# A gated delta stage with projections of 256 columns and a copy of them on the chip

## The chip, the cores and the metric

The kernel is one decoder layer for one sequence of 4096 tokens with a width of 1024, in float32, on one core of a Trainium2 chip. The metric is the device time of one execution in microseconds (us). TensorE multiplies matrices into PSUM; VectorE (DVE), ScalarE (ACT) and GpSimd (POOL) do the rest; GpSimd works in SBUF alone here; SyncE (SP) issues most DMAs.

## The reference, cut to what matters

The layer normalises the input, projects it, mixes the tokens by two kinds of heads (retention, and a gated delta rule), projects back, and runs a mixture of experts. The change touches the projections of the gated delta heads and the short convolution behind them:

```python
def causal_dwconv(x, w):          # CONV_WIDTH = 4 taps per channel, over time
    k = w.shape[0]
    return lax.conv_general_dilated(x, w[:, None, :].astype(x.dtype), window_strides=(1,), padding=((k - 1, 0),),
                                    dimension_numbers=('NWC', 'WIO', 'NWC'), feature_group_count=x.shape[-1])

h = modulate(rmsnorm(x, norm1_w[l]), shift1, scale1)
proj = h @ w_in[l]                # d_q, d_k, d_v: 512 columns each of the result
qkv = jax.nn.silu(causal_dwconv(jnp.concatenate([d_q, d_k, d_v], axis=-1), conv_w[l]))
cq, ck, cv = jnp.split(qkv.astype(jnp.float32), 3, axis=-1)
dn = gated_delta_rule(dq, dk, heads(cv, DN_HEADS), g, beta)   # dq, dk: cq, ck normalised per head
```

Each output of the convolution needs the projected value of its own token and of the three tokens before it; ahead of the first token stand zeros.

## The kernel before, in words

The kernel runs in four phases. `phase_a` makes the conditioning rows and the normalised, transposed activations, and computes the retention heads. It writes the activations to two tensors in device memory, `hh_d` and `hl_d` (a high part and the rest; a product is three matmuls: high x high, high x low, low x high). These have 4 columns more than tokens; the first 4 are filled with zeros from the tile `z4` (lines 276 to 279). `phase_b`, the stage of the change, computes the gated delta heads. `phase_c` applies the gates, the output projection and the router, `phase_d` the experts.

In `phase_b` the tokens go in 16 groups of G = 256, two chunks of 128 each. `dn_proj` does the projections of a group. The channels are on the partitions: 12 blocks of 128 channels (k, then q, then v), and for each block 24 matmuls (8 slices of the width by three products) accumulate in one PSUM tile `pjB`, with the weights stationary and the activations moving. The group's activations come from `load_h`: 8 DMAs per group into tiles under the tag "h" with 10 buffers, 260 columns each, that is the 256 tokens of the group and 4 columns ahead of them. The projection is thus computed for 260 columns, and the convolution reads its four shifted windows of 256 columns straight from PSUM: ScalarE scales two of them (lines 527 and 528), VectorE multiplies and adds the other two (line 530), GpSimd adds the last two partial sums (line 532), and after two blocks ScalarE applies Silu (line 537). There are three PSUM tiles under the tag "pj".

`dn_early` and `dn_late` do the delta rule of a group. `dn_early` makes the decay (`ru` on GpSimd, `pd` on TensorE, `dt`), the products of the keys (`pG`), and the inverse of the triangular matrices, of which 31 steps of two operations each run on VectorE (lines 600 and 602). Its blocks pass through device memory (`dgo`, `dgi`). `dn_late` combines the inverse blocks (`px`) and carries the state from chunk to chunk (`pP`, `pu`, `pkv`, `poB`).

The order of the work: the generators of a group are cut into steps, and `PROJ`, `EARLY` and `LATE` give each step a place, 12 places per group, so that the late steps of a group lie beside the projections of the next. That is the order in which the program is written. The final order on each engine is made by the framework's scheduler, which works through this program with a simulated timeline; each engine then runs its list strictly in order, and waits are semaphores. A tile with one buffer is written again when all readers of its last content are through.

Of the kernel before, what the change touches and what calls it, by code (L numbers as in the profile page):

```python
# [9 lines left out]
F32 = mybir.dt.float32  # L10
# [3 lines left out]
AF = mybir.ActivationFunctionType  # L14
ALU = mybir.AluOpType
# [4 lines left out]
P = 128  # L20
D = 1024
KD = D // P
H = 4
EPS = 1e-6
NE = 32
G = 256
GT = G // P
# [26 lines left out]
class Kern:  # L54
# [150 lines left out]
    def phase_a(self):  # L205
        tc, nc, T = self.tc, self.nc, self.T
        with tc.tile_pool(name="A", bufs=2) as p, ExitStack() as sctx:
# [21 lines left out]
            for g in range(self.NG):  # L229
                tiles = range(g * GT, (g + 1) * GT)  # L230
                if (g * GT) % 4 == 0:
                    n = min(4, self.NT - g * GT)
# [14 lines left out]
                for k2 in range(KD // 2):  # L247
                    pt = self.psum([P, 2, G], "pt", "tp")
                    for a in range(2):
                        for j, t in enumerate(tiles):  # L250
                            k = 2 * k2 + a
                            nc.tensor.transpose(pt[:, a, j * P:(j + 1) * P], xs[t][:, k * P:(k + 1) * P], self.ident)
                    hf = p.tile([P, 2, G], F32, name="hf", bufs=2)
                    for a in range(2):
                        k = 2 * k2 + a
                        nc.vector.tensor_scalar(hf[:, a], pt[:, a], self.sc1[:, k:k + 1], self.sh1[:, k:k + 1],
                                                op0=ALU.mult, op1=ALU.add)
# [5 lines left out]
                b = (g - min(2, self.NG - 8 // nb)) * nb  # L263
# [9 lines left out]
            nc.tensor.transpose(pc[:, :48], cwr, self.ident[:48, :48])  # L273
            self.cw = self.cp.tile([P, 4, 12], F32, name="cw")
            nc.vector.tensor_copy(self.cw, pc[:, :48].rearrange("p (w b) -> p w b", w=4))
            z4 = p.tile([P, KD, 4], F32, name="z4", bufs=1)
            nc.vector.memset(z4, 0.0)
            for d in (self.hh_d, self.hl_d):
                nc.sync.dma_start(d[:, 0:4].rearrange("(k p) n -> p k n", p=P), z4)

            self.bw = {nm: self.wblock(wi[:, c:c + 512], nc.sync) for nm, c in (("k", 2560), ("q", 2048), ("v", 3072))}
            sctx.close()
# [161 lines left out]
    def phase_b(self):  # L444
        tc, nc, T = self.tc, self.nc, self.T
        with tc.tile_pool(name="B", bufs=2) as p:
            wp = p
            hh0 = self.load_h(p, 0)

            def scalars():  # L450
                self.dn_scalars(p, p)
                self.Sd = p.tile([P, H, P], F32, name="Sd", bufs=1)
                nc.vector.memset(self.Sd, 0.0)
                self.Vb = self.wtile("Vb", F32)[:, 0:D].rearrange("p (h i) -> p h i", h=GT * H)
                nc.gpsimd.memset(self.Vb, 0.0)
                self.Tb = p.tile([64, 2 * H, 64], F32, name="Tb", bufs=1)
                nc.gpsimd.memset(self.Tb, 0.0)
                self.dgo = [self.dp.tile([32, 1024], F32, name=f"dgo{i}") for i in range(2)]
                self.dgi = [self.dp.tile([32, 1024], F32, name=f"dgi{i}") for i in range(2)]
                yield  # L460

            def next_weights():
                wi = self.w_in[0]
                self.gz = []
                for c in (1536, 3584):
                    self.gz.append(self.wblock(wi[:, c:c + 512], nc.sync))
                    yield
                self.dnw = self.xp.tile([P, 1], F32, name="dnw", bufs=1)
                nc.sync.dma_start(self.dnw, self.dn_norm_w.rearrange("o p -> p o"))
                self.wo = [self.wo_block(0)]  # L470
                yield

            steps = [(2.5, 0, 0, 0, scalars())]
            nw = next_weights()
            steps += [(12 * self.NG + 1 + i, 3, 0, i, nw) for i in range(3)]
            st_ = {}
            for g in range(self.NG):
                st_[g] = {}
                for kind, gen, at in ((2, self.dn_proj(p, g, st_[g], None if g else hh0), self.PROJ),
                                      (1, self.dn_early(p, g, st_[g]), self.EARLY),  # L480
                                      (0, self.dn_late(p, g, st_[g]), self.LATE)):
                    for i, o in enumerate(at):
                        steps.append((12 * g + o, kind, g, i, gen))
            for s in sorted(steps, key=lambda s: s[:4]):
                next(s[4], None)
# [11 lines left out]
    def load_h(self, p, g):  # L497

        nc = self.nc
        n = G + 4  # L500
        hh, hl = [], []
        for k2 in range(KD // 2):
            for dst, src, nm in ((hh, self.hh_d, "hhB"), (hl, self.hl_d, "hlB")):
                a = self.xp.tile([P, 2, n], F32R, name=nm, tag="h", bufs=10)
                nc.sync.dma_start(a.bitcast(F32), src[2 * k2 * P:(2 * k2 + 2) * P, g * G:g * G + n].rearrange(
                    "(a p) n -> p a n", p=P))
                dst += [a[:, 0], a[:, 1]]
        return hh, hl

    def dn_proj(self, p, g, st, hh=None):  # L510

        nc = self.nc
        hh, hl = hh or self.load_h(p, g)
        yield
        for b2 in (2, 3, 0, 1, 4, 5):
            cv = self.xp.tile([P, 2, G], F32, name="cv", tag="x0", bufs=2)
            for a in range(2):
                b = 2 * b2 + a
                pj = self.psum([P, G + 4], "pjB", "pj")
                for k in range(KD):  # L520
                    wh, wl = (w[:, b % 4 * P:(b % 4 + 1) * P] for w in self.bw["qkv"[b // 4]][k])
                    nc.tensor.matmul(pj, wh, hh[k], start=(k == 0), stop=False)  # L522
                    nc.tensor.matmul(pj, wh, hl[k], start=False, stop=False)  # L523
                    nc.tensor.matmul(pj, wl, hh[k], start=False, stop=(k == KD - 1))  # L524
                w = [self.cw[:, i, b:b + 1] for i in range(4)]
                t0 = p.tile([P, G], F32, name="cv0", bufs=2)
                nc.scalar.activation(cv[:, a], pj[:, 4:4 + G], AF.Copy, scale=w[3])
                nc.scalar.activation(t0, pj[:, 1:1 + G], AF.Copy, scale=w[0])  # L528
                for i in (2, 1):
                    nc.vector.scalar_tensor_tensor(cv[:, a], pj[:, 1 + i:1 + i + G], w[i], cv[:, a], op0=ALU.mult,  # L530
                                                   op1=ALU.add)
                nc.gpsimd.tensor_tensor(cv[:, a], cv[:, a], t0, op=ALU.add)  # L532
                if a == 0:
                    yield
            nm = "qkv"[b2 // 2] + "T"
            st[nm, b2 % 2] = o = p.tile([P, 2, G], F32, name=nm, bufs=4)
            nc.scalar.activation(o, cv, AF.Silu)
            yield

    def dn_early(self, p, g, s):  # L540
        nc = self.nc
# [5 lines left out]
        for c in range(GT):  # L547
# [9 lines left out]
            nc.gpsimd.tensor_tensor(dt[c], dt[c], self.ui[:, None, :].to_broadcast(sh), op=ALU.mult)  # L557
            s["dt", c] = dt[c]
            yield
        sk = p.tile([P, GT, H], F32, name="sk", bufs=2)  # L560
        for c in range(GT):
            pG.append(self.psum(sh, "pG", "tp"))
            for h in range(H):
# [8 lines left out]
        rk, irk, b, nb = (p.tile([P, GT, H], F32, name=n, bufs=2) for n in ("rk", "irk", "b", "nb"))  # L572
# [6 lines left out]
        for c in range(GT):  # L579
            for h in range(H):  # L580
                nc.vector.scalar_tensor_tensor(at[:, 4 * c + h], pG[c][:, h], nb[:, c, h:h + 1], dt[c][:, h],
                                               op0=ALU.mult, op1=ALU.mult)
# [14 lines left out]
        for j in range(31):  # L597
            n, m = j // 4 + 1, 31 - j
# [11 lines left out]
    def dn_late(self, p, g, s):  # L610
        nc = self.nc
# [6 lines left out]
        fl = lambda t: t.rearrange("p c h -> p (c h)")  # L618
        V, T, at = self.Vb, self.Tb, s["at"]
        kt, vv, sq, o = {}, {}, {}, {}  # L620
        rq = p.tile([P, GT, H], F32, name="rq", bufs=2)
        ms = p.tile([P, GT, H], F32, name="msB", bufs=2)

        def f_sq(c):
# [962 lines left out]
```

## Time and profile before

| What | us |
|---|---|
| Median of 3 runs (lowest, highest) | 4122.11 (4122.01, 4122.9) |
| The profiled execution's own time | 4121.5 |
| Span of the profile | 4119.7 |
| TensorE busy in the span (share) | 3911.6 (95%) |
| VectorE busy (share) | 2467.8 (60%) |
| ScalarE busy (share) | 1587.3 (39%) |
| GpSimd busy (share) | 1525.5 (37%) |
| Mean granted TensorE clock | 0.981 of full speed |

All times within the profile count from the start of the span. The gated delta stage lies from about 787 to 1725 us. An engine counts as busy while an instruction of it runs. Matmuls overlap: the recorded duration of one is longer than the distance to the start of the next, and a busy TensorE is a stream without gaps, not one at its peak. "Idle before" is the time in which an engine had nothing to run, and the name behind it is what ended it.

### The profile page before, as it was taken

What the parts mean: (1) busy time and instruction counts of PE and PEld (TensorE: products, weight loads), DVE (VectorE), ACT (ScalarE), POOL (GpSimd) and SP (SyncE); (2) the same over time, 40 slices, a digit from 0 to 9 for tenths busy, and PEclk for the clock granted to TensorE, in tenths of its full rate; (3) what the DMA queues carried; (4) which work ended last, traced back from release to release, by engine and by line L of the source; (5) the groups of instructions that cost most, each with busy time, mean ns of one, the idle gap of its engine ahead of it and who ended that gap; (6) DMA issues with size and microseconds to landing.
All of it is one profiled execution on the core that took longest, in us unless ns stands there. A gap on an engine that the chain in (4) does not pass through costs nothing.

```text
span 4119.7 us, 73091 instructions
## 1 busy us (share of the span) xinstructions
PE 3911.6 (95%) x27074; PEld 3515.6 (85%) x27074; DVE 2467.8 (60%) x6437; ACT 1587.3 (39%) x3298; POOL 1525.5 (37%) x2133
## 2 busy tenths in 40 slices
PE   5999999999999999979999999699999999999997
PEld 4888889899999999968888888598888888888886
DVE  6555543577778777742222222557777777777785
ACT  3433443444544444421122211234444444444453
POOL 2333334234443344222333333433333443454442
PEclk9999999999999999989999999799999999999999
DMA  6443322422222222453333333346666675666673
GB/s 194 137 128 123 98 91 89 115 59 74 58 60 66 74 61 60 118 158 120 118 123 123 123 123 111 119 142 209 204 225 226 216 237 193 232 209 206 225 233 125
DMA packets 459759, 577.48 MB, mean 140 GB/s; under 512 B 97296, under 2 KB 361720, under 8 KB 459400
## 3 DMA queue, kind: packets, MB, share of 16 engines
q1 hardware_dynamic: 411112, 464.72, 36.4%
q0 software_dynamic: 45632, 102.64, 7.4%
q10 hardware_dynamic: 2656, 5.42, 0.4%
q8 instruction: 214, 3.51, 0.4%
q14 instruction: 145, 1.19, 0.1%
HBM read 458.94 MB, written 166.78 MB: 152 GB/s over the span
## 4 chain that ended last, share of the span: by engine, by line
PE 77%; DVE 8%; DMA 8%; issue 3%; ACT 2%; SPq 1%; POOL 1%; DVEq 0%; POOLq 0%; ACTq 0%
PE ph L1410 5%; PE ph L1411 5%; PE ph L1409 5%; PE pjB L523 4%; PE pjB L522 4%; PE pjB L524 4%; PE py L1502 3%; PE py L1503 3%; PE py L1504 3%; PE pgz L291 3%; PE pgz L292 3%; PE pgz L290 3%; PE poC L291 3%; PE poC L292 3%; PE poC L290 3%
## 5 line engine op out<-in xcount | busy, mean ns | idle before, releaser
L1410 PE MATMUL ph<-xl,whD 128*128 128x240 f32 (+7 forms) x2048 | 588.2, 288 | 3.5 <-DVE xl L72 3.2
L1409 PE MATMUL ph<-xh,whD 128*128 128x240 f32 (+7 forms) x2048 | 580.1, 289 | 11.6 <-DVE ssD L1330 6.5
L1411 PE MATMUL ph<-xh,wlD 128*128 128x240 f32 (+7 forms) x2048 | 586.4, 288 | 0.0
L71 ACT ACTIVATE whD<-rawD 128x1024 fp32r<-128x1024 f32 x384 | 400.9, 1056 | 316.0 <-PE py L1503 125.9
L72 DVE TENSOR_TENSOR wlD<-rawD,whD 128x1024 fp32r<-128x1024 f32 x384 | 460.9, 1218 | 35.1 <-ACT whD L71 33.2
L522 PE MATMUL pjB<-hhB,whi 128*128 128x260 f32 x1536 | 443.1, 291 | 9.5 <-DVE cv L530 4.2
L523 PE MATMUL pjB<-hlB,whi 128*128 128x260 f32 x1536 | 440.7, 288 | 6.3 <-DMA hlB<-hl_d 6.1
L524 PE MATMUL pjB<-hhB,wlo 128*128 128x260 f32 x1536 | 440.8, 288 | 0.0
L1409 PEld LDWEIGHTS ph<-xh,whD 128*128 128x128 f32 x2048 | 388.9, 191 | 17.6 <-DVE ssD L1330 7.1
L1410 PEld LDWEIGHTS ph<-xl,whD 128*128 128x128 f32 x2048 | 391.1, 191 | 8.2 <-DVE xl L72 5.3
L1411 PEld LDWEIGHTS ph<-xh,wlD 128*128 128x128 f32 x2048 | 390.9, 191 | 1.9
L522 PEld LDWEIGHTS pjB<-hhB,whi 128*128 128x128 f32 x1536 | 289.0, 189 | 13.9 <-DMA hhB<-hh_d 4.5
L523 PEld LDWEIGHTS pjB<-hlB,whi 128*128 128x128 f32 x1536 | 290.3, 189 | 10.7 <-DMA hlB<-hl_d 8.3
L524 PEld LDWEIGHTS pjB<-hhB,wlo 128*128 128x128 f32 x1536 | 290.1, 189 | 1.6
L532 POOL TENSOR_TENSOR cv<-cv,cv 128x256 f32<-128x256 f32 x192 | 142.0, 740 | 399.2 <-DVE Xd L602 140.5
L1502 PE MATMUL py<-whD,hh 128*128 128x512 f32 (+4 forms) x640 | 259.5, 405 | 12.4 <-DVE hh L69 7.6
L1503 PE MATMUL py<-wlD,hh 128*128 128x512 f32 (+4 forms) x640 | 252.8, 395 | 0.0
L1504 PE MATMUL py<-whD,hl 128*128 128x512 f32 (+4 forms) x640 | 245.9, 399 | 4.6 <-DVE hl L72 4.3
L946 DVE TENSOR_TENSOR xC<-poC,xC 128x512 f32<-128x512 f32 x64 | 44.2, 691 | 329.6 <-PE poC L292 329.6
L1537 POOL DMA_INDIRECT acc_d<-ag,to x80 | 112.2, 1403 | 345.9 <-DVE ag L1510 257.9
L530 DVE SCALAR_TENSOR_TENSOR cv<-pjB,cw,cv 128x256 f32<-128x256 f32 x384 | 183.1, 479 | 78.8 <-ACT cv L528 71.5
L290 PE MATMUL pj<-whi,hh 128*128 128x512 f32 x512 | 205.8, 402 | 6.0 <-ACT whi L71 6.0
(449 smaller groups left out, 10234.4 us busy)
## 6 DMA issues: line engine op xcount, KB each, us to landing
rawD<-in_w_dram SPq DMA_DIRECT2D x384, 512.0 KB
wa<-in_w_ada_dram SPq DMA_DIRECT2D x48, 512.0 KB
hhB<-hh_d SPq DMA_DIRECT2D x64, 260.0 KB
hlB<-hl_d SPq DMA_DIRECT2D x64, 260.0 KB
acc_d<-xC SPq DMA_DIRECT2D x32, 520.0 KB
wraw<-in_w_in_dram SPq DMA_DIRECT2D x32, 512.0 KB
hh_d<-hh SPq DMA_DIRECT2D x16, 1024.0 KB
hl_d<-hl SPq DMA_DIRECT2D x16, 1024.0 KB
```

Source lines behind the costliest of these rows:

```text
L71: nc.scalar.activation(hi, src, AF.Copy)
L72: (e_lo or nc.vector).tensor_tensor(lo, src, hi.bitcast(F32) if hasattr(hi, "bitcast") else hi, op=ALU.subtract)
L290: nc.tensor.matmul(out, a, hi, start=(k == 0), stop=False)
L522: nc.tensor.matmul(pj, wh, hh[k], start=(k == 0), stop=False)
L523: nc.tensor.matmul(pj, wh, hl[k], start=False, stop=False)
L524: nc.tensor.matmul(pj, wl, hh[k], start=False, stop=(k == KD - 1))
L1409: nc.tensor.matmul(ph[nm], hi, xh[:, k, 0:n], start=(k == 0), stop=False)
L1410: nc.tensor.matmul(ph[nm], hi, xl[:, k, 0:n], start=False, stop=False)
L1411: nc.tensor.matmul(ph[nm], lo, xh[:, k, 0:n], start=False, stop=(k == KD - 1))
L1502: nc.tensor.matmul(py[i], a, hi, start=(k == 0), stop=False)
L1503: nc.tensor.matmul(py[i], a, lo, start=False, stop=False)
L1504: nc.tensor.matmul(py[i], b, hi, start=False, stop=(k == 3))
```

## The change

The projection is computed for the group's own 256 tokens. The last three projected columns of each block are kept in the tile `tail` (12 blocks of 3 columns) for the next group; it starts as zeros. Each PSUM tile is copied once by ScalarE into a tile `pjs` in SBUF with one buffer, behind three columns that GpSimd copies in from `tail`; GpSimd then copies the last three columns out to `tail`. The four windows of the convolution are read from `pjs`. The zero columns in device memory are no longer written, `load_h` reads 256 columns, and the small tiles `sk` and `rq` have one buffer in place of two.

```diff
@@ phase_a
-            z4 = p.tile([P, KD, 4], F32, name="z4", bufs=1)
-            nc.vector.memset(z4, 0.0)
-            for d in (self.hh_d, self.hl_d):
-                nc.sync.dma_start(d[:, 0:4].rearrange("(k p) n -> p k n", p=P), z4)
@@ phase_b
             hh0 = self.load_h(p, 0)
+            self.tail = p.tile([P, 12, 3], F32, name="tail", bufs=1)
+            nc.gpsimd.memset(self.tail, 0.0)
@@ load_h
-        n = G + 4
+        n = G
...
-                nc.sync.dma_start(a.bitcast(F32), src[2 * k2 * P:(2 * k2 + 2) * P, g * G:g * G + n].rearrange(
+                nc.sync.dma_start(a.bitcast(F32), src[2 * k2 * P:(2 * k2 + 2) * P, 4 + g * G:4 + g * G + n].rearrange(
@@ dn_proj
-                pj = self.psum([P, G + 4], "pjB", "pj")
+                pj = self.psum([P, G], "pjB", "pj")
...
                 w = [self.cw[:, i, b:b + 1] for i in range(4)]
+
+                pjs = p.tile([P, G + 4], F32, name="pjs", bufs=1)
+                nc.gpsimd.tensor_copy(pjs[:, 1:4], self.tail[:, b])
+                nc.scalar.activation(pjs[:, 4:], pj, AF.Copy)
+                nc.gpsimd.tensor_copy(self.tail[:, b], pjs[:, G + 1:])
                 t0 = p.tile([P, G], F32, name="cv0", bufs=2)
-                nc.scalar.activation(cv[:, a], pj[:, 4:4 + G], AF.Copy, scale=w[3])
-                nc.scalar.activation(t0, pj[:, 1:1 + G], AF.Copy, scale=w[0])
+                nc.scalar.activation(cv[:, a], pjs[:, 4:4 + G], AF.Copy, scale=w[3])
+                nc.scalar.activation(t0, pjs[:, 1:1 + G], AF.Copy, scale=w[0])
                 for i in (2, 1):
-                    nc.vector.scalar_tensor_tensor(cv[:, a], pj[:, 1 + i:1 + i + G], w[i], cv[:, a], op0=ALU.mult,
+                    nc.vector.scalar_tensor_tensor(cv[:, a], pjs[:, 1 + i:1 + i + G], w[i], cv[:, a], op0=ALU.mult,
                                                    op1=ALU.add)
@@ dn_early
-        sk = p.tile([P, GT, H], F32, name="sk", bufs=2)
+        sk = p.tile([P, GT, H], F32, name="sk", bufs=1)
@@ dn_late
-        rq = p.tile([P, GT, H], F32, name="rq", bufs=2)
+        rq = p.tile([P, GT, H], F32, name="rq", bufs=1)
```

## Rows read from the trace of the kernel before

**Rows 1.** Windows: span, busy of PE, PEld, DVE, ACT, POOL, clock, DMA.
```profile
787.00:1725.00 938.00, 911.78 (x8529) 882.62 (x8529) 708.05 (x2485) 449.98 (x1147) 367.76 (x578) 1.00 0.26 71
...
1300.00:1600.00 300.00, 298.92 (x2841) 290.65 (x2840) 228.68 (x815) 142.23 (x375) 121.06 (x194) 1.00 0.25 68
```

**Rows 2.** Timeline of TensorE: start, duration, line, output, operands; firsts and lasts.
```profile
809.07 0.28 PE L524 MATMUL pjB<-hhB,wlo 128*128 128x260 f32 x1
...
823.33 0.28 PE L523 MATMUL pjB<-hlB,whi 128*128 128x260 f32 x1
...
2712.03 0.40 PE L1409 MATMUL ph<-xh,whD 128*128 128x256 f32 x2
...
2734.38 0.28 PE L1411 MATMUL ph<-xh,wlD 128*128 128x256 f32 x1
...
2891.47 0.28 PE L1439 MATMUL ph<-wlD,xh 128*128 128x256 f32 x1
...
2897.15 0.28 PE L1438 MATMUL ph<-whD,xh 128*128 128x256 f32 x1
```

**Rows 3.** Waits of TensorE in the stage: us in total, times, longest.
```profile
PE pjB L523 <- DMA hlB<-hl_d: 6.1, 8, 2.4
PE pjB L522 <- DVE cv L530: 4.2, 1, 4.2
PE pjB L522 <- DMA hhB<-hh_d: 3.9, 6, 1.0
PE pG L564 <- DVE dt L650: 2.7, 2, 2.2
```

**Rows 4.** Chain of waits around 800 us: start, us, what.
```profile
799.68 0.48 ACT cv L527
...
804.51 0.40 DVE cv L530
...
805.05 0.36 PE pjB L522
```

**Rows 5.** Windows again, the stretch behind that wait.
```profile
803.00:809.00 6.00, 3.95 (x20) 3.98 (x21) 4.73 (x11) 5.41 (x8) 1.42 (x2) 0.72 0.70 197
```

**Rows 6.** Groups by line and shape, ScalarE: count, busy us, mean ns, idle before.
```profile
L527 ACT ACTIVATE cv<-pjB,cw 128x256 f32<-128x256 f32 x192 | 91.0, 474 | 158.3 <-PE pjB L524 157.5
...
L1414 ACT ACTIVATE hs<-ph 128x256 f32<-128x256 f32 x36 | 13.7, 380 | 35.5 <-PE ph L1411 35.3
...
L71 ACT ACTIVATE hh<-hs 128x256 fp32r<-128x256 f32 x27 | 11.3, 417 | 61.2 <-DVE hs L1415 55.6 <-DVE rb_t L435 5.7
```

**Rows 7.** Waits in the stage, all engines.
```profile
ACT cv L527 <- PE pjB L524: 157.5, 103, 4.6
```

**Rows 8.** Groups by line and shape, VectorE.
```profile
L530 DVE SCALAR_TENSOR_TENSOR cv<-pjB,cw,cv 128x256 f32<-128x256 f32 x384 | 183.1, 479 | 78.8 <-ACT cv L528 71.5 <-POOL dt L557 4.4 <-issue 0.2
...
L1415 DVE TENSOR_TENSOR hs<-ph,hs 128x256 f32<-128x256 f32 x36 | 15.2, 422 | 62.8 <-PE ph L1411 55.3 <-issue 7.5
...
L72 DVE TENSOR_TENSOR hl<-hs,hh 128x256 fp32r<-128x256 f32 x36 | 15.2, 421 | 5.3 <-ACT hh L71 4.8
```

**Rows 9.** Timeline of VectorE and GpSimd in one group.
```profile
1210.79 1.04 POOL L552 TENSOR_TENSOR ru<-K,lah 128x512 fp32r<-128x512 f32 x1 [0.75 <-PE pq L657]
...
1211.08 0.85 DVE L602 TENSOR_TENSOR Xd<-Xd,Ltmp 128x76 f32<-128x76 f32 x1
...
1211.85 0.68 DVE L752 TENSOR_TENSOR o<-poB,o 128x512 f32<-128x512 f32 x1
```

**Rows 10.** Line 602: least, median, greatest ns; then its group in the stage.
```profile
L602 DVE TENSOR_TENSOR Xd<-Xd,Ltmp x496: 159/216/1205, 851.5 to 1761.3; 128x60 f32<-128x60 f32 x16, 128x28 f32<-128x28 f32 x12, 128x66 f32<-128x66 f32 x11, 128x48 f32<-128x48 f32 x10
...
L602 DVE TENSOR_TENSOR Xd<-Xd,Ltmp 128x60 f32<-128x60 f32 (+24 forms) x474 | 130.1, 274 | 11.2
```

**Rows 11.** Groups by line and shape, GpSimd.
```profile
L435 POOL TENSOR_TENSOR rb_t<-rb_y 128x8 f32<-128x8 f32 x45 | 9.3, 206 | 6.1 <-DVE rb_y L432 4.1
...
L532 POOL TENSOR_TENSOR cv<-cv,cv 128x256 f32<-128x256 f32 x192 | 142.0, 740 | 399.2 <-DVE Xd L602 140.5 <-DVE cv L530 114.5 <-DVE Ltmp L600 101.0
```

**Rows 12.** Timeline of SyncE: the zero fill.
```profile
23.99 1.98 SPq L279 DMA_DIRECT2D hl_d<-z  x1
```

## The prediction

> **What bounds the kernel now.** I read the busy time by stage first. The gated delta stage runs from 787 to 1725 us. TensorE is busy for 911.8 of its 938 us, and for 298.9 of 300 us in its middle, at the full granted clock; VectorE follows with 708, ScalarE with 450, GpSimd with 368 [rows 1]. The stage therefore ends when TensorE has worked off its stream, and an edit counts if it shortens that stream or makes it wait. A projection block is 24 matmuls, and there are 12 blocks in each of 16 groups: 192 blocks, 4608 matmuls, one block per 938 / 192 = 4.89 us.
>
> [...] At the end of the first group 120 projection matmuls of 260 columns start between 809.07 and 823.33: 14.26 / 119 = 119.8 ns each [rows 2]. A bare block is thus 24 x 0.12 = 2.9 us, and the other 2 us of a block are the small matmuls of the delta rule.
>
> Last the waits. TensorE waits little in this stage: 6.1 and 3.9 us for the activation loads, 4.2 us once for the convolution, 2.7 us for dt; nothing else on VectorE costs more than 2 us [rows 3].
>
> **The shorter matmul.** The expert stage has matmuls of 256 columns with the same arrangement (weights stationary, activations moving): 192 of them start from 2712.03 to 2734.38, 22.35 / 191 = 117.0 ns. With activations stationary, 49 start from 2891.47 to 2897.15, 118.3 ns [rows 2]. So 4 columns are worth 1.5 to 2.8 ns, or 4608 x that: 6.9 to 12.9 us. The first kind is ours, so I take 2.8 ns, on the 97% of the stage in which TensorE is busy: **-12.5 us**. The number of matmuls and weight loads stays.
>
> **The first wait.** The 4.2 us wait is one event. Three PSUM buffers are full at the start of the stage. ScalarE reads the first at 799.68, but the buffer is free only after VectorE's second tap, and TensorE goes on at 805.05 [rows 4]. It resumes at the lower of the clock's two levels for a while: the granted clock is 0.72 over 803 to 809, 6 x 0.28 = 1.7 us of full speed lost after that idle time [rows 5]. After the change ScalarE's copy frees the buffer. The next copy has to wait for VectorE's second tap of the first block, so one more block fits in and then it stops again: I take one block, **-3 us**, with ends 0 and -(4.2 + 1.7) = -5.9. Next late there are the second column block's weights, which are converted in the same microseconds.
>
> **ScalarE.** It gains 192 copies from PSUM. An unscaled 128x256 activation out of PSUM took 380 ns: 73 us. The two scaled taps (474 ns) now read SBUF; an unscaled activation of that size from SBUF took 417 ns, so I add 37 ns to each of 384: 14 us [rows 6]. ScalarE goes from 450 to 537 of 938 us. It now waits 157.5 us for TensorE at exactly this place [rows 7]; that idle time covers the copies. Without this cover, 0.45 us per block would stand in the loop below.
>
> **VectorE.** The 384 taps keep their number and shape (479 ns); a two-input operation of that size took 422 ns with one input in PSUM and 421 ns with both in SBUF [rows 8]. By length alone I take 0. [...]
>
> But both inputs now lie in SBUF, and there VectorE and GpSimd disturb each other. At 1211.08 an operation of the triangular inverse with both inputs in SBUF takes 0.85 us and ends just after GpSimd's operation of 1210.79 to 1211.83, while the one at 1211.85, which reads PSUM, takes its usual 0.68 us beside GpSimd's next [rows 9]. Line 602 has a median of 216 ns and a mean of 274 ns: 58 ns of such waiting per operation [rows 10]. For 384 taps: 22 us. The ends: 0 (today's taps wait for nothing of the kind), and half a GpSimd operation (740 / 2 ns) for each tap that meets a busy GpSimd (0.39 of the stage): 55 us. [...]
>
> **GpSimd.** It gains 384 copies of 128x3. Its nearest row is 128x8 with 206 ns: 79 us, 368 to 447 of 938 us; it idles 399 us ahead of the convolution's last addition today [rows 11]. These copies lock out VectorE as well, which raises the 55 us to 384 x 0.48 x 370 = 68 us.
>
> **The added waits.** There is one buffer of the copy. The copy of block b waits for the second tap of block b-1, and behind it in ScalarE's queue stand the taps, Silu and the small PSUM reads that TensorE's inverse steps wait for. GpSimd's copy-in waits for the same, behind the addition of block b-1 (0.74 us); both taps wait for it. The loop per block is copy 0.38 + scaled tap 0.51 + two taps 0.96, with hops some 2.1 us; by GpSimd 0.74 + 0.21 + 0.96, 1.9 us and hops. Both are under 2.9 us, the densest pace of TensorE, and far under 4.89, and TensorE has three PSUM buffers ahead of it. VectorE with 730 of 938 us is not the bound either. What comes through are its lateness in the inverse chain and the steps behind it: I take that TensorE's waits for VectorE, ScalarE and GpSimd, some 5 us without the loads and the first wait, double: **+5 us**, with ends 0 and +23 (VectorE's whole 22 us).
>
> **Nothing each:** the dropped zero fill goes out at 24 us, where no one waits for it (2 us of the DMA queue, so 0 to -2) [rows 12]. The loads stay 8 per group, 256 KB in place of 260, on the same queue in the same order. sk and rq with one buffer are written again only after their last reader on VectorE.
>
> **Sum:** 4121.5 us of the profiled execution (4119.7 span, 1.8 around it) - 12.5 - 3 + 5 = 4111.0. The median of the runs is 0.6 above the profiled one: **4112 us**.
>
> **Rivals.** (1) The lock eats the gain: 4121.5 - 12.5 - 3 + 14 = 4120. For it: the inverse chain (two times 31 operations per group) already carries 58 ns each, and the 24 taps of a group, many of which stand between them, now add 1.4 us; if two thirds of that, 0.9 us, stands in front of each group's inverse steps on TensorE, it is 14 us. Against it: in 300 us of the middle TensorE waits 1.1 us in all, so there is slack that no view gives in numbers. (2) Slower: the single copy ties ScalarE and GpSimd to VectorE. Where VectorE works on the inverse chain, it reaches the taps late; ScalarE then stands at the copy, and behind it the reads that TensorE's inverse needs, and GpSimd at its copy-in with the inputs of pd behind it. Price: half a block, 1.5 us, in each of 16 groups, +24, and no gain at the start: 4121.5 - 12.5 + 24 = 4133. It decides from the point where the loop with all that stands in the queues passes a block's 4.89 us. Against it: the bare loop is 2.1 us. (3) The columns are worth nothing because the stream is held by the weight loads: 4121.5 - 3 + 5 = 4124. Against it: the two distances of rows 2. (4) The earlier release of PSUM also takes away small waits: 4121.5 - 12.9 - 5.9 + 1 = 4104.
>
> **Chances.** Forecast 0.46, its own range 4105 to 4117; rival 1 0.28, rival 2 0.16, rival 3 0.05, rival 4 0.05. A measurement of this kernel tells about 0.2% (8 us) from no change: faster is under 4113.9, slower over 4130.4. Of the forecast 0.41 lies below, 0.05 above: faster 0.41 + 0.05 = 0.46, same 0.05 + 0.28 + 0.05 = 0.38, slower 0.16. The range is 4102 to 4134; half of rivals 2 and 4 is left out.
>
> **What would show it.** Right: 117 to 118 ns from start to start in the projections, no 4 us wait near 800 us, TensorE busy for 97% of a stage of some 927 us. Wrong: a mean of the taps well above 540 ns, new rows of TensorE waiting for the inverse's operands (rival 1), ScalarE's copy waiting for the taps and TensorE for the copy (rival 2), or an unchanged distance (rival 3).

## The result, and the profile after

The changed kernel took 4156.29 us (median of 6 runs, 4147.4 to 4165.54), the kernel before 4122.5 on the same chip: a ratio of 1.0082, 95% interval 1.0069 to 1.0094. It is 34 us slower; 10 us faster was forecast, and the range ended at 4134.

The profiled execution (4165.54 us, span 4163.5) is the slowest of the six; it shows the loss in the changed stage. From the first to the last projection matmul it took 958.0 us (787.8 to 1745.8) against 926.1 before (787.9 to 1713.9). The other 12 of the 44 us by which the span grew lie behind it. There the two kernels do the same work, and in the kept traces of the other versions (e6 aside) this rest takes 2384 to 2410 us, 2406 before and 2418 here; so these 12 us can't be laid to the change.

Windows of the changed kernel (columns as in [rows 1]): the whole stage, which is 32 us longer now, then the stretches shown of before, then one just behind a wait.
```profile
787.00:1757.00 970.00, 915.29 (x8443) 881.90 (x8444) 750.88 (x2462) 552.12 (x1341) 437.55 (x962) 0.98 0.24 66
787.00:1725.00 938.00, 890.42 (x8214) 858.32 (x8215) 728.30 (x2383) 537.80 (x1313) 423.09 (x930) 0.99 0.24 64
1300.00:1600.00 300.00, 286.81 (x2654) 277.16 (x2652) 231.43 (x764) 173.27 (x426) 137.32 (x305) 0.98 0.22 62
803.00:809.00 6.00, 4.20 (x33) 3.81 (x32) 4.95 (x11) 4.25 (x9) 3.35 (x6) 1.00 0.53 164
1235.80:1239.40 3.60, 3.60 (x20) 3.60 (x19) 3.56 (x17) 0.67 (x3) 2.18 (x6) 0.53 0.00 0
```
TensorE now idles 970 - 915.3 = 54.7 us of its stage, where it idled 938 - 911.8 = 26.2 [rows 1], 28.5 us more. In the middle, once all but free of waits (298.9 of 300), it idles 13 us. The low clock near 803 us (0.72 over 803 to 809 [rows 5]) is gone, it is 1.00 there now, and others have come.

Timeline of TensorE in the changed kernel (start, duration, line, output, operands; in brackets the idle time before and what ended it).
```profile
1232.06 0.28 PE L521 MATMUL pjB<-hlB,whi 128*128 128x256 f32 x1
...
1233.00 0.28 PE L520 MATMUL pjB<-hhB,whi 128*128 128x256 f32 x1
1235.25 1.55 PE L567 MATMUL pG<-kT 128*128 128x128 f32 x8 [1.97 <-DVE dt L653]
...
1236.81 0.41 PE L522 MATMUL pjB<-hhB,wlo 128*128 128x256 f32 x1
...
1238.95 0.41 PE L520 MATMUL pjB<-hhB,whi 128*128 128x256 f32 x1
```
Nine matmuls lie between 1232.06 and 1233.00: 0.94 / 8 = 117.5 ns from start to start, the distance that was forecast for 256 columns; over the whole stage its median fell from 120 to 118 ns, and the mean over undisturbed stretches from 119.9 to 118.4. Behind the wait of 1.97 us eleven lie between 1236.81 and 1238.95, 214 ns each: the granted clock is 0.53 over those 3.6 us, and 0.50 from 1235.9 to 1239.2; the traces of both kernels have it at 1.00 or at 0.50, nowhere between. That costs 3.6 us x 0.47 = 1.7 us on top of the wait. From the first to the last projection matmul the kernel before had one such stretch, this one has nine: some 15 us in all, 14 more than before. Each lies behind a wait of 1.2 to 2.1 us or behind two shorter ones; three of the nine waits are for the loads of the activations, and not every wait is followed by such a stretch (one of 1.99 us at 874 us and one of 1.3 us at 886 us are not).

Waits in the changed kernel's stage: first TensorE's (to set beside [rows 3]), then the longest of the other engines (beside [rows 7]).
```profile
PE pG L567 <- ACT dt L559: 9.0, 9, 2.1
PE pG L567 <- DVE dt L653: 5.8, 4, 2.0
PE pjB L520 <- ACT pjs L527: 5.6, 7, 1.3
PE pd L557 <- POOL tail L528: 5.0, 3, 1.7
PE px L684 <- DVE Tb L677: 6.1, 4, 1.9
...
POOL cv L535 <- DVE cv L533: 132.7, 81, 5.6
POOL tail L528 <- ACT pjs L527: 120.9, 53, 8.1
ACT pjs L527 <- DVE cv L533: 88.1, 56, 5.7
ACT pjs L527 <- PE pjB L522: 41.4, 24, 3.9
ACT pjs L527 <- DVE Ltmp L603: 19.6, 13, 3.8
```
The 4.2 us wait at the start of the stage has gone; in its place there are seven of up to 1.3 us, for the copy, six of them up to 830 us. The waits before pG, pd and px, the small matmuls of the delta rule, were 8 us in all and are 29 (some smaller rows included). Of the kernel before, with the 2.7 us of [rows 3]:
```profile
PE pd L554 <- ACT dt L556: 2.1, 3, 1.3
PE px L681 <- DVE Tb L674: 1.5, 2, 1.2
PE pG L564 <- ACT dt L556: 1.1, 1, 1.1
```
And ScalarE, which waited 157.5 us for TensorE at the convolution, waits 41 us for it and over 100 us for VectorE's taps and inverse: the idle time that the prediction counts as cover for the copies is no longer there as such.

Groups of the changed kernel by line and shape in its stage (beside [rows 6, 8, 10, 11]), then VectorE's taps and inverse.
```profile
L530 ACT ACTIVATE cv<-pjs,cw 128x256 f32<-128x256 f32 x191 | 97.1, 508 | 4.8
L531 ACT ACTIVATE cv<-pjs,cw 128x256 f32<-128x256 f32 x191 | 95.9, 502 | 5.3 <-POOL pjs L526 4.1
L527 ACT ACTIVATE pjs<-pjB 128x256 f32<-128x256 f32 x192 | 73.7, 384 | 197.5 <-DVE cv L533 88.1 <-PE pjB L522 41.4 <-DVE Ltmp L603 19.6
...
L528 POOL COPY tail<-pjs 128x3 f32<-128x3 f32 x192 | 41.3, 215 | 125.6 <-ACT pjs L527 120.9
L526 POOL COPY pjs<-tail 128x3 f32<-128x3 f32 x192 | 37.0, 193 | 0.0
...
L533 DVE SCALAR_TENSOR_TENSOR cv<-pjs,cw,cv 128x256 f32<-128x256 f32 x382 | 215.6, 564 | 90.9 <-ACT cv L530 66.8 <-POOL pjs L526 9.9 <-POOL rb_t L431 7.7
L605 DVE TENSOR_TENSOR Xd<-Xd,Ltmp 128x60 f32<-128x60 f32 (+24 forms) x465 | 135.9, 292 | 11.3
```
The taps went from a mean of 479 to 564 ns. Least, median and greatest of them:
```profile
L533 DVE SCALAR_TENSOR_TENSOR cv<-pjs,cw,cv x382: 385/484/2055, 802.2 to 1750.8; 128x256 f32<-128x256 f32 x191
```
The median hardly moved (481 before): most taps are no slower, and some take up to four times as long. I read that as waiting for GpSimd: the 47 taps of over 600 ns, 31.5 us above the median together, all lie beside a GpSimd operation of over 600 ns, and those that lie beside no operation of it take at most 489. Where one input is in PSUM no tap takes over 486 ns (the kernel before, with 87 of them beside such an operation) or 487 (e12).

VectorE and GpSimd ahead of the wait of 1.97 us before pG, in the changed kernel.
```profile
1231.46 1.29 DVE L605 TENSOR_TENSOR Xd<-Xd,Ltmp 128x54 f32<-128x54 f32 x1
1232.68 0.47 DVE L533 SCALAR_TENSOR_TENSOR cv<-pjs,cw,cv 128x256 f32<-128x256 f32 x1
...
1234.52 0.68 DVE L653 TENSOR_TENSOR dt<-pQ,dt 128x512 f32<-128x512 f32 x1
...
1231.27 1.42 POOL L560 TENSOR_TENSOR dt<-dt,K 128x512 f32<-128x512 f32 x1
```
TensorE's pQ was through at 1229.9. VectorE reads it at 1234.52, 4.6 us later, because eleven instructions of the inverse and the convolution stand ahead, one of which takes 1.29 us beside a GpSimd operation in place of some 0.22. The other operand, `dt`, is of the group before and long ready. Until this read is done, the PSUM buffer that pG needs is taken.

### The profile page after: what moved, and what is told of

It is laid out like the page before. It is cut to its first block, busy times and chain, and to the rows that moved or that the text cites. A ratio compares the mean times of both kernels' runs of the same rounds, so it can differ in the third digit from the quotient of the medians.

```text
span 4163.5 us, 73959 instructions
## 1 busy us (share of the span) xinstructions
PE 3932.3 (94%) x27074; PEld 3529.8 (85%) x27074; DVE 2517.9 (60%) x6436; ACT 1696.2 (41%) x3504; POOL 1597.1 (38%) x2518
## 4 chain that ended last, share of the span: by engine, by line
PE 52%; DVE 8%; DMA 6%; issue 3%; ACT 1%; SPq 1%; POOL 1%; DVEq 0%; POOLq 0%; ACTq 0%
PE ph L1413 5%; PE ph L1412 5%; PE ph L1414 5%; PE pgz L287 3%; PE pgz L288 3%; PE pgz L286 3%; PE py L1505 3%; PE py L1506 3%; PE poC L287 3%; PE poC L286 3%; PE poC L288 3%; PE py L1507 3%; DVE wlD L72 2%; PE pl L982 1%; PE pjB L521 1%
## 5 line engine op out<-in xcount | busy, mean ns | idle before, releaser
L520 PE MATMUL pjB<-hhB,whi 128*128 128x256 f32 x1536 | 443.1, 291 | 10.0 <-ACT pjs L527 5.6
L521 PE MATMUL pjB<-hlB,whi 128*128 128x256 f32 x1536 | 445.2, 291 | 4.0 <-DMA hlB<-hl_d 3.9
L522 PE MATMUL pjB<-hhB,wlo 128*128 128x256 f32 x1536 | 440.2, 288 | 0.0
L533 DVE SCALAR_TENSOR_TENSOR cv<-pjs,cw,cv 128x256 f32<-128x256 f32 x384 | 216.6, 564 | 91.3 <-ACT cv L530 67.2
```

## The experiments

The ratios are to the kernel before on the same chip, with 95% intervals.

| version | ratio | interval |
|---|---|---|
| the change | 1.0082 | 1.0069 to 1.0094 |
| e1 256 columns, halo in PSUM, no copy | 1.0059 | 1.0037 to 1.0080 |
| e2 260 columns, copy | 1.0117 | 1.0092 to 1.0142 |
| e3 change, two copy buffers | 1.0070 | 1.0053 to 1.0086 |
| e4 change, tail on ScalarE | 1.0063 | 1.0046 to 1.0079 |
| e5 before, sk and rq single | 1.0038 | 1.0023 to 1.0052 |
| e7, e8 before, other places | 1.0010, 1.0006 | 0.9994 to 1.0026, 0.9991 to 1.0022 |
| e9 change, two rq | 1.0081 | 1.0054 to 1.0108 |
| e10 as e1, two rq | 1.0011 | 0.9997 to 1.0025 |
| e11 as e2, two rq | 1.0071 | 1.0047 to 1.0094 |
| e12 as e11, taps on PSUM | 1.0039 | 1.0020 to 1.0058 |
| e13 as e4, two rq | 1.0092 | 1.0075 to 1.0110 |
| e14 as e13, two copy buffers | 1.0065 | 1.0052 to 1.0078 |
| e15 as e10, tail stored later | 1.0053 | 1.0039 to 1.0067 |
| e16 as e15, halo ahead of the matmuls | 1.0032 | 1.0023 to 1.0042 |
| e17 as e16 but for group 0 | 1.0017 | 1.0007 to 1.0027 |
| e18 as e17, halo on VectorE | 1.0026 | 1.0016 to 1.0036 |

**First round: which part of the change.** A "halo" is the three columns ahead of a group's own. Three theories: L, the lock, which is here the waiting of a VectorE operation with both inputs in SBUF beside a GpSimd operation (0.85 us [rows 9] against a median of 0.22 [rows 10]); S, the single copy buffer; G, GpSimd's small copies.

e1 takes the copy away:
```diff
-pjs[:, 1:4] <- tail (GpSimd); pjs[:, 4:] <- pj (ScalarE); tail <- pjs (GpSimd)
+nc.scalar.activation(pj[:, 1:4], self.tail[:, b], AF.Copy)
+nc.scalar.activation(self.tail[:, b], pj[:, G + 1:], AF.Copy)
```


> Keeps the 256 columns and the kept tail, drops the copy in SBUF: the PSUM tile has 260 columns, the matmuls write the last 256, ScalarE writes the three kept columns into PSUM in front of them and copies the last three out; all taps read PSUM as in the kernel before. Theory L (VectorE's taps with two SBUF inputs wait for GpSimd), theory S (the single SBUF copy ties ScalarE and GpSimd to VectorE) and theory G (GpSimd's 384 small copies) all remove their cause here, so each expects the gain of the shorter matmuls alone: 192 x 24 x 2 ns = 9 us, 4110 to 4118. If the time stays near 4155, the cause is in what all versions with 256 columns share (the load without the halo, the kept tail, the order that the scheduler makes).

e2 makes the copy alone, on the kernel before:
```diff
+pjs = p.tile([P, G + 4], F32, name="pjs", bufs=1)
+nc.scalar.activation(pjs, pj, AF.Copy)      # the four taps read pjs; sk, rq single
```


> The kernel before with the copy alone: 260 columns, ScalarE copies all 260 into one SBUF buffer, the taps read it; no kept tail, no copies on GpSimd, sk and rq with one buffer. Theory L: VectorE's taps go from 479 to some 560 ns, nearly all of the loss is here, and the gain of the columns is missing: 4155 to 4170. Theory S: the single buffer is here, but without GpSimd in its loop: 4140 to 4160. Theory G: no loss, 4120 to 4128.

e3 and e4 change one thing in the changed kernel:
```diff
+if a == 1: pjs = self.xp.tile([P, 512], F32, name="pjs2", tag="sg", bufs=1)[:, 0:G + 4]   # e3
-nc.gpsimd.tensor_copy(...)                  # e4: both small copies
+nc.scalar.activation(..., AF.Copy)
```


> The changed kernel with two copies in SBUF in place of one (the second lies in the place of a tile that only the next stage uses). Theory S: ScalarE's waits for the taps (118 us in the profile after) go, and with them the loss: 4112 to 4125. Theory L: the taps keep their 560 ns, 4145 to 4160. Theory G: as L, 4145 to 4160.

> The changed kernel with the 384 copies of three columns on ScalarE instead of GpSimd (ScalarE gains some 75 us of busy time in the stage). Theory G: the loss goes, 4112 to 4125. Theory L: the taps meet GpSimd less often (its busy share of the stage falls from 0.45 to 0.37), a fifth of the loss goes: 4145 to 4155. Theory S: unchanged or a little worse by ScalarE's longer loop, 4150 to 4170.

Measured: 1.0059, 1.0117, 1.0070, 1.0063. The times expected above go by the chip of the result, where the kernel before takes 4122.5 us; it takes 4111.6 where these four ran, so they are read here as ratios to 4122.5. The copy alone is worse than the whole change, as L expected, and L's ranges hold in e3 and e4, too. But S missed in e2 and e3, G in e2 and e4, and all three missed in e1, which has neither copy nor GpSimd work and still lost 24 us. All four share something that I had not looked at.

**Second round: work or order.** Either the added work costs (W), or any edit lets the scheduler lay another, worse order (O).
```diff
-sk = p.tile(..., name="sk", bufs=2)   rq = p.tile(..., name="rq", bufs=2)
+sk = p.tile(..., name="sk", bufs=1)   rq = p.tile(..., name="rq", bufs=1)      # e5
+nc.tensor.matmul(pj[:, 4:], wh, hh[k][:, 4:], ...)     # e6, all three products; taps read pj[:, 4:4 + G]
+EARLY = [3.25, 4.25, 6.25, 6.75, 7.25, 8.25, 9.25, 10.25, 11.25]     # e7: each + 0.25
+LATE = [s[0] + 0.25 for s in LATE_]                                  # e8
```


> The kernel before, with the two small buffers sk and rq single, as the change has them, and nothing else. W (the work that the change adds on ScalarE, VectorE and GpSimd makes the loss) expects no change, 0 to +4 us: no instruction is added. O (each edit gives every engine another order of instructions, and the order of the kernel before happens to leave TensorE no wait in the groups of 1240 to 1714 us, where an edited one brings a wait back in every group) expects anything from 0 to +25 us, and waits on TensorE that come back each 58 us.

> The kernel before with its 4608 matmuls of the stage on 256 columns instead of 260, and nothing added: no tail, no copy. It leaves out the shift of the convolution (all four taps read the same 256 columns). W expects the gain that the matmuls' spacing gives, 4608 x 2 to 2.8 ns = 9 to 13 us less than the kernel before. O expects that gain in the spacing, and from 0 to 25 us of new waits on TensorE, so -12 to +15 us.

> The kernel before with the nine early places at which a piece of the chunk work is let in behind a projection block a quarter of a block later; the instructions and their number are the same. W expects -3 to +3 us. O expects a change of +8 to +40 us.

> The kernel before with the late places a quarter of a block later; the instructions and their number are the same. W expects -3 to +3 us. O expects a change of +8 to +40 us, if not here then in the run with the early places moved.

These two other orders alone are worth +2 to +4 us, within the error (e7, e8), where O expected 8 to 40: O in its strong form fell. e5 adds no instruction and loses 16 us, so W (0 to 4) missed there. e6 leaves out the shift of the convolution. Its total (4425 us) can't be read: other values send the tokens to other experts, whose stage loads 468 weight blocks in place of 384. Its projections are nominally shorter and took 935.4 us against 926.1 to 937.5 in the kernels with 260 columns and no copy: no gain to be seen, though one of less than that spread would not show.

The trace shows what one rq changes. pq, the PSUM tile that rq is computed from, is read when the one rq is free, that is after the last step of the group before (msB). The kernel before in one group, then e5 in the same group:
```profile
1324.61 1.84 PE L657 MATMUL pq<-one,sqq 128*128 128x1 f32 x16
...
1328.40 0.16 DVE L659 TENSOR_SCALAR rq<-pq 128x8 f32<-128x8 f32 x1
```
```profile
1328.50 0.28 PE L657 MATMUL pq<-one,sqq 128*128 128x1 f32 x2
...
1335.33 0.30 DVE L757 SCALAR_TENSOR_TENSOR msB<-msB,rq 128x8 f32<-128x8 f32 x1 [0.32 <-ACT jk L755]
...
1335.76 0.15 DVE L659 TENSOR_SCALAR rq<-pq 128x8 f32<-128x8 f32 x1
...
1345.25 1.16 PE L564 MATMUL pG<-kT 128*128 128x128 f32 x8 [2.10 <-ACT dt L556]
```
From pq's last matmul to rq it is 2 us before and 7 us in e5; over the 16 groups, counted from the start of that matmul, 0.3 to 3.6 against 2.0 to 11.9, and 2.9 to 12.9 in the changed kernel (6.9 or more in 15 of them). So long one of the two PSUM buffers that pd, pG, pQ, pq and the transposes share is taken. No instruction waits for rq itself, so no wait bears its name. The last row is a wait that this group doesn't have in the kernel before; that it follows from the late reading of pq, nine us earlier, is argued. In e5's kept trace, that of its fastest execution, the stage takes 931.8 us, 5.7 more than before; the rest of the 16 us is not to be seen in it.

**Third round: rq double again (R), and what the copy costs by itself (C).**
```diff
-rq = p.tile(..., name="rq", bufs=1)
+rq = p.tile(..., name="rq", bufs=2)     # e9: the change; e10: e1 (sk too); e11, e12: e2
+nc.vector.scalar_tensor_tensor(cv[:, a], pj[:, 1 + i:1 + i + G], ...)     # e12: taps on PSUM
```


> The changed kernel with rq double, as it was before the change; sk stays single. R (with one rq VectorE may read the PSUM tile pq of a group only after the last step of the group before has read rq: 6.9 to 12.9 us after its last matmul in the changed kernel against 0.3 to 3.6 us before, and so long one of the two PSUM buffers of the chunk work is lost to TensorE) expects pq read within 4 us again, fewer waits of TensorE before pG, pd and ptv, and 8 to 20 us less than the changed kernel: a ratio to the kernel before of 1.003 to 1.006. C (the copy on ScalarE and the taps on two SBUF operands make the whole loss) expects the ratio of the changed kernel, 1.007 to 1.009.

> The version with 256 columns and the halo written into PSUM (no copy, taps on PSUM), now with sk and rq double. R expects its three waits per group on TensorE to go and the ratio to fall from 1.0059 to 0.998 to 1.002. If what costs there is the halo's 384 small copies on ScalarE, the ratio stays at 1.004 to 1.007.

> The kernel before (260 columns, no tail) with the copy into one SBUF buffer, as in the second experiment, but rq double. R and C together expect 1.0117 less the 0.0038 that the single buffers alone cost: 1.006 to 1.009, the price of the copy by itself. If the single rq had been all, 1.000 to 1.003; if the copy were all, 1.011 to 1.013.

> The run before this one with VectorE's two taps reading the projection in PSUM; the copy is still made and ScalarE's two taps read it. The lock (VectorE instructions with both inputs in SBUF wait for GpSimd's) expects the taps back at a mean of 479 ns and most of the copy's price gone: 1.000 to 1.003. If it is ScalarE's added 73 us and later releases, the ratio stays where the run before this one is, 1.006 to 1.009.

Two rq gave back 0.0048 in e10 (with sk) and 0.0046 in e11, 19 us each, near the 16 of e5 (0.0038), and both ratios lie where R expected them. In the changed kernel they gave 0.0001, though pq is read within 0.3 to 5.3 us there: R missed in e9. The copy by itself costs 1.0071, 29 us; with the two taps on PSUM 1.0039 is left, between the two expectations. The taps of e11, then of e12:
```profile
L532 DVE SCALAR_TENSOR_TENSOR cv<-pjs,cw,cv 128x256 f32<-128x256 f32 x382 | 204.9, 536 | 110.7 <-ACT cv L529 104.1 <-POOL rb_t L440 3.1 <-POOL ru L554 0.5
```
```profile
L532 DVE SCALAR_TENSOR_TENSOR cv<-pjB,cw,cv 128x256 f32<-128x256 f32 x384 | 183.9, 480 | 109.3 <-ACT cv L529 105.6 <-issue 0.2
```
The lock is gone from the taps (536 to 480 ns), and with it 13 us (0.0032, by the two intervals 0.0002 to 0.0062). In e12 ScalarE alone frees the copy, too, and VectorE frees PSUM again, so this is the lock and the release by VectorE together.

**Fourth round: what ends last in the changed kernel; can the columns pay?**
```diff
# e13: e9 with the small copies on ScalarE (as e4); e14: and the second copy buffer (as e3)
# e15: e10, tail <- pj behind the two ScalarE taps; e16: and pj[:, 1:4] <- tail ahead of the matmuls
```


> The changed kernel with rq double and the two small copies of the tail on ScalarE. If GpSimd's 384 copies are what ends last there (they hold the lock against the taps and keep the adds of the taps late), the ratio falls from 1.0081 to 1.001 to 1.005. If it is the single copy buffer, or VectorE's queue whatever GpSimd does, it stays at 1.006 to 1.009.

> As the run before, with a second copy buffer in space that is free in this stage. If the single copy buffer ends last, this falls below the run before by 0.002 or more, to 1.000 to 1.004; if it is the lock and ScalarE's added copy, it stays within 0.001 of the run before. The lock's and ScalarE's share that the copy on 260 columns showed (1.0071), less what the columns give (0.002), puts it at 1.005.

> 256 columns, halo in PSUM, rq and sk double; ScalarE keeps the last three columns after its two taps instead of ahead of them. VectorE's taps can start 206 ns earlier, and so the PSUM tile comes free. If ScalarE's small copies on the path of the taps eat the columns' gain of 9 us: 0.997 to 1.000. If they cost by ScalarE's time as a whole: 1.000 to 1.002, as in the tenth run.

> As the run before, and the halo is written into PSUM ahead of the projection's matmuls, so that neither small copy lies between the last matmul and the taps. If the path matters: 0.996 to 0.999. But ScalarE now waits for the free PSUM tile (the taps of a block before) with other work queued behind; if that decides, 1.002 to 1.010.

e13 excludes GpSimd's copies as what holds e9 (1.0092). The second buffer gave 0.0027 (e14; by the intervals 0.0005 to 0.0049), half of what it would have to give as the one cause; the fall was in the range expected for the single buffer, the ratio that is left was not. e15 missed by far: one small instruction moved behind two others in the same queue cost 0.0042. e16 (1.0032) came out in the second of its ranges, that for a ScalarE that waits for the free tile. It starts late, because the halo of the first blocks stands behind ScalarE's work for the stage before:
```profile
PE pjB L521 <- ACT pjB L518: 10.4, 1, 10.4
```

**Last round.**
```diff
+if g > 0: nc.scalar.activation(pj[:, 1:4], self.tail[:, b], AF.Copy)     # ahead of the matmuls; e18: nc.vector.tensor_copy
+if g == 0: nc.scalar.activation(pj[:, 1:4], self.tail[:, b], AF.Copy)    # behind them
```


> As the run with the halo ahead of the matmuls, but in group 0, where the stage before still fills ScalarE's queue, the halo is written behind them. If the late start (first projection matmul at 800.9 in place of 786 us) is what costs there: 1.0032 less 8 to 13 us of 4110, so 1.000 to 1.0012. If the first group had made it up by itself (its pq ends at 855.3 us as in the kernel before): 1.002 to 1.004.

> As the run before, with the halo from group 1 on written by VectorE right behind its own taps of the block that had the PSUM tile before, so that ScalarE waits for no free tile. If ScalarE's blocked queue (it waits 106 us for VectorE's taps at the halo's place) costs TensorE its 11 us before pG, the columns' gain shows: 0.996 to 0.999. If VectorE's added 180 copies (a chain of up to 30 us on the engine that bounds the chunk work) take it back: 1.001 to 1.006.

e17 got 6 us back (by the intervals 0 to 12), between its two expectations. e18 came out as feared for VectorE's added copies (180 of 159 ns): it was no faster than e17. No version with 256 columns beat the kernel before; e10 alone can't be told from it.

## Why the prediction was wrong

**The shorter matmul** was right in kind: 2.0 to 2.3 ns by medians and single stretches, 1.5 by the mean over undisturbed stretches, in place of 2.8. That makes 7 to 11 us less stream, inside the ends of 6.9 and 12.9. It bought nothing that the time shows: with no copy and two rq, 256 columns came to 1.0011 to 1.0053 (e10, e15 to e18). These versions also carry 384 small copies for the halo, most of them on ScalarE, which may eat the gain (174 to 178 ns each on ScalarE in e15 and e16, 159 on VectorE in e18). Or, in the kernel before, TensorE's stream and the chain of a group through ScalarE, VectorE and the two PSUM buffers end nearly together, so that a shorter stream meets the chain. Both are argued from those runs; neither is shown by itself.

**The first wait** went, but its 3 us did not come: the stream was 6.5 us ahead of the kernel before after four blocks, 1.2 us after 12 and level after 24, because the waits for the copy followed, 5.6 us in seven parts.

**The sizes of the parts** were right: the copy 384 ns (380 taken), ScalarE's taps 502 and 508 (511), GpSimd's copies 78 us (79), the taps' waiting 382 x (564 - 479) = 32 us (22 taken, ends 0 and 68). The taps' mean is 564 ns in the change and 536 in e11, and 479 and 480 where one input is in PSUM (the kernel before, e12). The end of 68 counted GpSimd's copies among what the taps wait for. The trace doesn't show that: the 38 taps that lie beside those copies alone take at most 491 ns. By length alone nothing was taken for a tap that leaves PSUM, and so it came: a median of 481 ns before and 484 after.

**The step that failed is the one on the added waits:** "Both are under 2.9 us ... I take that TensorE's waits ... double: +5 us". Its base was too small: without the loads and the first wait, TensorE's waits for the other engines, all of over 0.15 us added up from the trace, were 10 us before, not 5. And they did not double: counted alike (up to the last projection matmul, without the waits for the copy), they are 35 us in the changed kernel, 25 more. The loop was summed bare, each operation alone on its engine, and compared with the pace of TensorE. In the trace each stands behind its engine's other work: ScalarE's copy waits 88 us for taps that stand behind the inverse, and VectorE's reads of the small matmuls' PSUM stand behind the inverse, the taps and operations that wait for GpSimd (pQ, 4.6 us). The clock behind these waits was left out: behind nine waits TensorE ran at a clock of 0.50 for 3.4 us each time, some 14 us more, which the 7 to 11 us shorter stream offsets in part. The signs of rivals 1 and 2 both came (taps of 564 ns, TensorE waiting for the inverse's operands, ScalarE's copy waiting for taps). Rival 2 had the mechanism's direction (+24 us, by the single copy buffer), but that buffer is a part: 5 us in e3, within the error, and 11 in e14.

By their ratios the versions sort by where the taps read: all eight whose taps read the copy lie at 1.0063 to 1.0117, all ten whose taps read PSUM and whose total can be read, down to the moved places, at 1.0006 to 1.0059. The border is not sharp: the intervals of e1 (to 1.0080) and e4 (from 1.0046) overlap, and so do the lengths of the stage in the kept traces (943 to 974 us, and 919 to 950). All eight also carry the copy itself; e11 and e12 are the one pair that keeps the copy and moves only VectorE's taps.

**"sk and rq with one buffer are written again only after their last reader"** was true and was costed at nothing; on the kernel before it cost 16 us by itself (e5). What was overlooked is what the late writer still holds: PSUM. In the changed kernel a second rq gave nothing (e9), so how much of the 34 us is due to it stays open.

**What stays open.** The parts don't add up one by one. Two rq are worth 16 to 20 us in three versions and nothing in the two with copy and tail together (e9; e13 against e4 is even 0.0029 worse). And a moved small instruction was worth 0.0042 (e15). Shown are TensorE's added waits and where they lie in the changed kernel; the worth of the taps' place (e12 against e11) and of the single rq in versions where copy and tail don't come together; and that neither GpSimd's copies nor the copy buffer alone is the cause. How the 34 us divide between lock, release, ScalarE's lateness and the order of the instructions is not shown. That the taps' lock alone was taken away, with the copy still released by VectorE, wasn't tried.

## What to carry to other kernels

Sum a loop with the queues that its operations stand in, not by their bare durations, and where several engines share two PSUM buffers ask for each edit who reads PSUM later now. A buffer made single can cost without a wait that bears its name: look at what its writer holds while it waits for its turn. Where the busiest engine idles 3%, a shorter stream on it may be worth its difference only if the chain beside it has slack (argued here, not shown), and small edits of the order move the time by as much: an edit worth under 0.4% can't be judged from one version.

## What the runs showed of the hardware

The wait of 1.97 us before pG cost TensorE nearly 4 us (1.97 + 1.7): behind it the matmuls of 256 columns lay 214 ns apart in place of 117.5, at a granted clock of 0.53. One of 1.99 us at 874 us was followed by no lower clock. GpSimd's copy of three columns took 193 to 215 ns (the means of its two lines), as long as its 128x8 operation of [rows 11] (206 ns): three columns were no cheaper than eight. VectorE's copy of three columns took 159 ns (e18). An operation of VectorE's inverse with both inputs in SBUF, line 605 with a median of 216 ns, took 1.29 us beside a GpSimd operation of 1.42 us.
